# Hybrid encoder layer: the Fourier projections moved ahead of the low-rank ones, the convolution last, and a third pair of tiles for split weights

## The chip, the cores and the metric

The kernel runs on one core of a Trainium2 chip. The metric is the time of one execution in device microseconds (us). One core has five engines that matter here, each with its own in-order queue of instructions: PE (TensorE, the matrix engine), DVE (VectorE), ACT (ScalarE), POOL (GpSimd) and SP (SyncE, which here issues DMA transfers). PEld is the loading of weights into PE, which overlaps its matmuls.

## The reference

One layer on 1024 positions of 1024 channels in float32. The normalised input is projected by `w_in` to 2048 columns, which go to four groups of heads; their results are joined, projected by `w_out`, and a SwiGLU block follows.

```python
def reference(x, ...):
    h = _layer_norm(x, ln0_g, ln0_b)
    p = h @ w_in                                   # 2048 columns
    p_ssm, p_rkv, p_conv, p_fft = jnp.split(p, [256, 1024, 1792], axis=-1)
    y_a = _s5_mixer(p_ssm, ...)                    # complex state space, a scan per direction, GELU, GLU
    y_b = _rwkv7_mixer(h, p_rkv, ...)              # delta-rule scan per direction
    y_c = _short_conv_mixer(p_conv, conv_w)        # bgate * conv3(cgate * xc)
    y_d = _fourier_mixer(p_fft)                    # Re(fft2) over positions and 64 channels
    y = jnp.concatenate([y_a, y_b, y_c, y_d], axis=-1)
    h = _layer_norm(ALPHA * h + y @ w_out, ln1_g, ln1_b)
    f = (silu(h @ ffn_w1) * (h @ ffn_w3)) @ ffn_w2
    return _layer_norm(ALPHA * h + f, ln2_g, ln2_b)

# inside _rwkv7_mixer, from the normalised input xn itself:
    w_lora = tanh(xw @ w1) @ w2        # xw, xa, xg: xn mixed with its neighbours
    a = sigmoid(a0 + (xa @ a1) @ a2)
    g = sigmoid(xg @ g1) @ g2
```

## The kernel before

A scheduler orders the instructions of each engine when the program is built. The Python code gives it two streams that run beside each other. `chain()` has priority: S5, then the preparation of the RWKV scan (`rwkv_first`: `rk_prep` for both directions and both halves of the heads, then `rk_inverse(0)`, the triangular inverse of the first direction), then the scan itself (`rk_scan`, 32 steps, 16 for each direction). `beside()` fills what the chain leaves free; its parts stand in a fixed order, so that a part later in it can only come after the parts ahead of it. Once placed, an instruction keeps its place in its engine's queue: an engine whose next instruction waits does nothing else meanwhile.

Before the two streams, `start()` normalises the input, writes it transposed into eight tiles (HA and HB, the rounded part and the remainder, each in halves), and projects four blocks of 128 columns, two for S5 and two of the RWKV keys.

A projection of 128 columns is one call of `block`: the weight is loaded into `wraw` (`load`, one tile), split into a rounded part `wh` (ACT, L399) and a remainder `wl` (POOL, L400), and multiplied in two halves of 512 positions, each 48 matmuls in groups of three (L161 to L163, tile `proj`). `split` has two buffers each for `wh` and `wl` (tags WH and WL).

The parts of `beside()`:

- `lora_project`: seven projections of low-rank weights. Each weight is first multiplied by a mixing vector on DVE (L909, tile `lmw`) and the difference taken on POOL (L924). The second projection of a pair is added to the first on DVE (L925, tile `la`).
- `rkv_project`: the four other blocks for RWKV (tiles p3).
- `conv` woven with `residuals`. `conv` does, for each of two blocks, the gate C, the value, and the gate B; its DVE operations are L431 (two, product with the gate), L434 and L436 (two taps) and L438 (two, product with the other gate). `residuals` multiplies the input out again (tile `res`, L1443) and writes it to DRAM (`d_res`, L1445), eight times, through three tiles Z0, Z1, Z2.
- `fourier_project`: two projections; the first half of both, then the second half of both, into tiles C1 and C2, then to DRAM (`d_z`).
- After these `h` is not read any more, and its tiles HA0, HB0, HA1, HB1 are used as `far` for the second direction of RWKV: `rwkv_second` loads rows back from DRAM into them (L993, tiles HA0f and HB0f; HA0f and HB0f stand in HA0 and HB0), builds diagonal blocks from them (L1135, tile `abd`), multiplies (L1138, tile `pa`) and then runs `rk_inverse(1)`.

`rk_inverse` builds `ua` (L1159), and runs a loop of substitutions in which DVE and POOL each do their share (L1180, L1182), transposes (L1193, tile `tj`), and multiplies blocks (L1217, tile `pm`); then scan steps can start (matmuls `px`, `pz`, `po`, `pc`; L1303 is `pz`). When the scan of the first direction is through its 16 steps, that of the second needs `rk_inverse(1)`. The order of the parts around the change is this:

```python
for part in (self.lora_project, self.rkv_project):
    yield from part()
yield from woven((self.conv(), 0), (self.residuals(), 0))
yield from self.fourier_project()
```

## Time and profile before

| | us |
|---|---|
| time, median of 3 runs | 1436.99 |
| lowest and highest | 1435.92 and 1444.51 |
| the profiled execution, its own time | 1439.41 |
| its span in the profile | 1437.7 |
| PE busy in the span | 1324.8 (92%) |
| DVE busy | 1065.7 (74%) |
| ACT busy | 635.4 (44%) |
| POOL busy | 544.5 (38%) |

The times that follow are counted from the start of the span. The profiled execution has 1.7 us outside its span and is 2.4 us above the median. A share of 92% is a mean over stages: PE is full from 828 us to the end and has its idle time ahead of that. The stages of the table of windows below are the start (to 74.5), S5 (to 281), the preparation of the scan (to 420), the substitutions (to 461.6), the first block products (to 481.9), the first direction's steps up to the second direction's first (to 588.5), the rest of the scan (to 828), and the Fourier, output and SwiGLU matmuls.

### The profile page before, as it was taken

To read this page: it belongs to the slowest core of one execution; us is meant where nothing else is said; L and a number is where in the kernel's file an instruction comes from. 1 tells how busy PE (TensorE), PEld (TensorE's weight loads), DVE (VectorE), ACT (ScalarE), POOL (GpSimd) and SP (SyncE) were. 2 spreads that over 40 slices of the span, in tenths; PEclk is the share of its full clock that TensorE was granted. 3 is DMA by queue.
4 is the path that set the end of the run, shared out by engine and by line. 5 is a ranking of instruction groups with operands and counts; after the bars stand their busy time and mean duration, and the time that the engine had idled before them with its cause. 6 is when DMAs were issued, how large, how long until landed. Compare 5 with 4: busy or idle time off the path is not lost.

```text
span 1437.7 us, 23997 instructions
## 1 busy us (share of the span) xinstructions
PE 1324.8 (92%) x9200; PEld 1203.7 (84%) x9200; DVE 1065.7 (74%) x1882; ACT 635.4 (44%) x1249; POOL 544.5 (38%) x513
## 2 busy tenths in 40 slices
PE   6968797978799998999998999999999999999997
PEld 5968796866698877778887999999999999888885
DVE  7996967377788588678787867667666664689688
ACT  4312052565533578564338544444444454432231
POOL 5467655043356352411237443333333331122006
PEclk9989898999799999999999999999999999999999
DMA  6121024114253202405421353344444448998552
GB/s 231 36 69 27 8 94 127 45 38 121 75 163 105 108 16 96 128 27 173 158 103 59 121 175 136 140 150 162 147 147 147 148 147 297 393 354 294 190 184 117
DMA packets 94980, 196.10 MB, mean 136 GB/s; under 512 B 24721, under 2 KB 47377, under 8 KB 94865
## 3 DMA queue, kind: packets, MB, share of 16 engines
q1 hardware_dynamic: 92976, 190.74, 39.0%
q10 hardware_dynamic: 1888, 3.82, 0.8%
q8 instruction: 73, 1.20, 0.3%
q14 instruction: 43, 0.34, 0.1%
HBM read 125.32 MB, written 68.16 MB: 135 GB/s over the span
## 4 chain that ended last, share of the span: by engine, by line
PE 54%; DVE 27%; ACT 7%; DMA 5%; issue 4%; POOL 1%; SPq 1%; DVEq 0%; ACTq 0%; POOLq 0%
PE f L161 4%; PE fx L161 4%; PE f L163 4%; PE f L162 4%; PE fx L163 4%; PE fx L162 4%; PE ops L161 2%; PE ops L162 2%; PE ops L163 2%; PE fy L161 2%; PE fy L162 2%; PE fy L163 2%; DMA fw<-w 2%; PE proj L161 2%; PE proj L162 2%
## 5 line engine op out<-in xcount | busy, mean ns | idle before, releaser
L161 PE MATMUL proj<-HA,wh 128*128 128x256 f32 x672 | 201.9, 301 | 15.3 <-DVE la L925 11.1
L163 PE MATMUL proj<-HA,wl 128*128 128x256 f32 x672 | 197.3, 294 | 2.9 <-POOL wl L400 2.9
L162 PE MATMUL proj<-HB,wh 128*128 128x256 f32 x672 | 197.7, 294 | 1.7 <-POOL HB L340 1.7
L161 PE MATMUL fx<-H,fc 128*128 128x256 f32 x672 | 187.2, 283 | 2.5 <-ACT fe L1673 1.8
L162 PE MATMUL fx<-H,fc 128*128 128x256 f32 x672 | 189.5, 282 | 0.0
L163 PE MATMUL fx<-H,fc 128*128 128x256 f32 x672 | 189.0, 282 | 0.0
L1391 POOL TENSOR_TENSOR fc<-fw,fc 128x512 fp32r<-128x512 f32 x88 | 125.0, 1422 | 166.7 <-ACT fc L1390 165.8
L161 PEld LDWEIGHTS proj<-HA,wh 128*128 128x128 f32 x672 | 132.5, 197 | 22.0 <-issue 11.1
L162 PEld LDWEIGHTS proj<-HB,wh 128*128 128x128 f32 x672 | 132.4, 197 | 7.0 <-issue 4.9
L163 PEld LDWEIGHTS proj<-HA,wl 128*128 128x128 f32 x672 | 132.4, 197 | 5.8 <-POOL wl L400 3.1
L161 PEld LDWEIGHTS fx<-H,fc 128*128 128x128 f32 x672 | 126.5, 190 | 3.6 <-ACT fe L1673 2.6
L162 PEld LDWEIGHTS fx<-H,fc 128*128 128x128 f32 x672 | 127.6, 190 | 0.1
L163 PEld LDWEIGHTS fx<-H,fc 128*128 128x128 f32 x672 | 127.6, 190 | 0.0
L161 PE MATMUL f<-fb,fa 128*128 128x512 f32 x276 | 108.8, 394 | 0.0
L163 PE MATMUL f<-fb,fa 128*128 128x512 f32 x276 | 108.8, 394 | 0.0
L162 PE MATMUL f<-fb,fa 128*128 128x512 f32 x276 | 108.6, 394 | 0.0
L161 PE MATMUL fy<-H,fc 128*128 128x256 f32 x336 | 94.3, 281 | 0.4 <-ACT fe L1671 0.4
L162 PE MATMUL fy<-H,fc 128*128 128x256 f32 x336 | 94.3, 281 | 0.0
L163 PE MATMUL fy<-H,fc 128*128 128x256 f32 x336 | 94.2, 280 | 0.0
L1390 ACT CAST fc<-fw 128x512 fp32r<-128x512 f32 x110 | 67.8, 621 | 32.3 <-POOL fc L1391 14.3
L1391 POOL TENSOR_TENSOR fc<-fs,fc 128x512 fp32r<-128x512 f32 x22 | 30.1, 1369 | 105.9 <-ACT fc L1390 104.6
L1390 ACT CAST fb<-fs 128x512 fp32r<-128x512 f32 x47 | 29.1, 623 | 92.3 <-PE f L163 59.7
(634 smaller groups left out, 3794.3 us busy)
## 6 DMA issues: line engine op xcount, KB each, us to landing
fa<-d_f SPq DMA_DIRECT2D x77, 512.0 KB, 4.3
d_f<-fg SPq DMA_DIRECT2D x70, 512.0 KB, 2.7
fw<-w SPq DMA_DIRECT2D x46, 512.0 KB, 3.7
fg<-w SPq DMA_DIRECT2D x44, 256.0 KB, 6.2
wraw<-w_in SPq DMA_DIRECT2D x16, 512.0 KB, 4.1
xt<-x SPq DMA_DIRECT2D x8, 512.0 KB, 8.3
d_res<-res SPq DMA_DIRECT2D x8, 512.0 KB, 3.0
oraw<-w_out SPq DMA_DIRECT2D x8, 512.0 KB, 3.6
```

Source lines behind the costliest of these rows:

```text
L161: mm(out, whi, xhi, start=start, stop=False, skip_group_check=shared)
L162: mm(out, whi, xlo, start=False, stop=False, skip_group_check=shared)
L163: self.last_mm = mm(out, wlo, xhi, start=False, stop=stop, skip_group_check=shared)
L1390: nc.scalar.copy(out=hi, in_=raw)
L1391: (eng or nc.gpsimd).tensor_tensor(out=lo, in0=raw, in1=hi.bitcast(F32), op=ALU.subtract)
```

## The change

Four edits. The order in `beside()` becomes Fourier, low-rank, RWKV, and the convolution with the residuals last. `split` takes its tiles in turn from three places, the two buffers of WH and WL and the tiles Z0 and Z1. `fourier_project` does block after block, into P4 and P5. `residuals` has only Z2 left.

```diff
@@ build: beside()
-                        for part in (self.lora_project, self.rkv_project):
+
+                        for part in (self.fourier_project, self.lora_project, self.rkv_project):
                             yield from part()
                         yield from woven((self.conv(), 0), (self.residuals(), 0))
-                        yield from self.fourier_project()
@@ split
         if to is None:
-            hi = self.m.tile([128, NK, 128], R, tag="WH", name=self.name("wh"), bufs=2)
-            lo = self.m.tile([128, NK, 128], R, tag="WL", name=self.name("wl"), bufs=2)
+
+            self.splits += 1
+            hi, lo = (self.t(tag, [128, NK, 128], name, R)
+                      for tag, name in zip((("WH", "WL"), ("WH", "WL"), ("Z0", "Z1"))[self.splits % 3], ("wh", "wl")))
@@ fourier_project
-        z = [self.t(f"C{1 + b}", [128, S], "fz") for b in range(2)]
-        parts = [self.block(self.load(14 + b), lambda n, ps, b=b: nc.scalar.copy(
-            out=z[b][:, n * 512:(n + 1) * 512], in_=ps)) for b in range(2)]
-        for n in range(2):
-            for part in parts:
-                yield next(part)
         for b in range(2):
-            nc.sync.dma_start(out=self.d_z[b], in_=z[b])
+            z = self.t(f"P{4 + b}", [128, S], "fz")
+            yield from self.block(self.load(14 + b), lambda n, ps: nc.scalar.copy(
+                out=z[:, n * 512:(n + 1) * 512], in_=ps))
+            nc.sync.dma_start(out=self.d_z[b], in_=z)
@@ residuals
-            x = self.t(f"Z{t % 3}", [128, 2, 4, 128], "res")
+            x = self.t("Z2", [128, 2, 4, 128], "res")
```

Since the scheduler places everything anew, the order on each engine is where the change is to be seen. In the rows below a line number is that of its own program; in the changed one most are one lower (L909 is L908, L925 is L924, L1180 is L1179), and L400 is L403, L993 is L992, L440 is L443.

**VectorE in the first part of S5.** The names: `s5x`, `s5w`, `s5tt` and `s5e` are tiles of S5, `lmw` the low-rank weight times its mixing vector. Before, from the 288th row of the queue:

```order
L511 TENSOR_TENSOR s5x_86_920<-s5qin_1117,s5x_93_927 128x512 x2
L512 TENSOR_TENSOR s5x_86_920<-s5qin_1118,s5x_93_927 128x512 x2
L519 TENSOR_TENSOR s5x_93_927<-s5x_93_927 128x256
L909 TENSOR_SCALAR lmw_1348<-lraw_1346,vec 128x64 x11
L520 TENSOR_TENSOR s5x_93_927<-s5x_93_927 128x256
L519 TENSOR_TENSOR s5w_921<-s5x_86_920 128x512
...
L520 TENSOR_TENSOR s5w_922<-s5x_86_920 128x512
L909 TENSOR_SCALAR lmw_1348<-lraw_1346,vec 128x64 x5
L520 TENSOR_TENSOR s5w_922<-s5x_86_920 128x512
```

The same place in the changed program:

```order
L510 TENSOR_TENSOR s5x_84_900<-s5qin_1100,s5x_91_907 128x512 x2
L511 TENSOR_TENSOR s5x_84_900<-s5qin_1101,s5x_91_907 128x512 x2
L518 TENSOR_TENSOR s5x_91_907<-s5x_91_907 128x256
L518 TENSOR_TENSOR s5w_901<-s5x_84_900 128x512
L519 TENSOR_TENSOR s5x_91_907<-s5x_91_907 128x256
```

and, twenty rows on, where two operations of L736 stand:

```order
L734 TENSOR_TENSOR s5x_84_900<-s5qout_1102,s5x_91_907 128x1152
L735 TENSOR_TENSOR s5x_84_900<-s5qout_1103,s5x_91_907 128x1152
L736 SCALAR_TENSOR_TENSOR s5x_91_907<-s5x_84_900 128x1152
L908 TENSOR_SCALAR lmw_1629<-lraw_1627,vec 128x64 x16
L736 SCALAR_TENSOR_TENSOR s5x_91_907<-s5x_84_900 128x1152
```

The sixteen operations of `lmw` for the second pair of low-rank weights (11 and 5) have left the place between S5's own operations and stand in one piece between the two of L736 (L737 before). The two `la` operations of L925, which stood before between L735 and the second L737, are gone from there too.

**GpSimd at the substitutions of the first inverse.** The rows of L1180 and L1182 are POOL's share of the loop. Before, the loop's first rows, its middle, and what follows its end:

```order
L1166 AFFINE_SELECT ti_4280<-ua_4279 128x1024
L400 TENSOR_TENSOR wl_3699<-wraw_3696,wh_3698 128x1024
L1180 TENSOR_TENSOR tpr_4281<-ua_4279,ti_4280 128x18
...
L1180 TENSOR_TENSOR tpr_4281<-ua_4279,ti_4280 128x8x11
L400 TENSOR_TENSOR wl_3823<-wraw_3820,wh_3822 128x1024
L1182 TENSOR_TENSOR ti_4280<-ti_4280,tpr_4281 128x8x11
...
L1182 TENSOR_TENSOR ti_4280<-ti_4280,tpr_4281 128x18
L400 TENSOR_TENSOR wl_3829<-wraw_3826,wh_3828 128x1024
```

In the changed program:

```order
L1165 AFFINE_SELECT ti_4280<-ua_4279 128x1024
L1179 TENSOR_TENSOR tpr_4281<-ua_4279,ti_4280 128x18
L403 TENSOR_TENSOR wl_3813<-wraw_3810,wh_3812 128x1024
L1181 TENSOR_TENSOR ti_4280<-ti_4280,tpr_4281 128x18
...
L1181 TENSOR_TENSOR ti_4280<-ti_4280,tpr_4281 128x3x16
L403 TENSOR_TENSOR wl_3938<-wraw_3935,wh_3937 128x1024
L1179 TENSOR_TENSOR tpr_4281<-ua_4279,ti_4280 128x2x17
```

Of three remainders of weights at the loop (one ahead of it, one in it, one behind it) two are left, both inside.

**SyncE between the end of the preparation and the first scan steps.** `cg` to `d_y` is a finished block of the convolution, `res` to `d_res` a residual, HA0f and HB0f the loads of the second direction, `ring` a load of the scan. Before:

```order
L405 DMA wraw_3820<-w_in 128x1024
L405 DMA wraw_3826<-w_in 128x1024
L440 DMA d_y<-cg_3444 128x1024
L993 DMA HB0f<-d_p 128x1024
L993 DMA HA0f<-d_p 128x1024 x2
...
L1362 DMA ring_4598<-d_b 128x2x128 x2
L453 DMA d_z<-fz_3818 128x1024
```

In the changed program:

```order
L408 DMA wraw_3935<-w_in 128x1024
L1444 DMA d_res<-res_3422 128x1024
L443 DMA d_y<-cg_3105 128x1024
L1444 DMA d_res<-res_3506 128x1024
L1444 DMA d_res<-res_3528 128x1024
L1361 DMA ring_4598<-d_b 128x2x128 x2
L992 DMA HB0f<-d_p 128x1024
L992 DMA HA0f<-d_p 128x1024 x2
```

The loads into HA0f and HB0f stand behind the scan's `ring` loads now; the last reader of HA0 and HB0 ahead of them is the first half of the last convolution block instead of the first half of the second Fourier block.

## Rows read from the trace of the kernel before

**Rows 1.** Table of windows: start and end of the stretch, its length, then busy time and number of instructions of PE, PEld, DVE, ACT and POOL, the granted clock of PE as a share of full speed, the share of DMA, and GB/s. The stages.

```profile
74.50:281.00 206.50, 170.13 (x1247) 158.70 (x1247) 149.81 (x246) 57.76 (x85) 109.93 (x104) 0.91 0.21 60
281.00:420.00 139.00, 115.62 (x734) 96.34 (x732) 108.99 (x109) 77.93 (x107) 48.88 (x27) 0.90 0.33 92
...
481.90:588.50 106.60, 95.94 (x681) 81.16 (x679) 79.67 (x219) 76.55 (x214) 41.87 (x87) 0.95 0.21 69
...
828.00:1437.70 609.70, 598.19 (x4160) 556.02 (x4158) 426.47 (x580) 240.40 (x423) 179.29 (x111) 0.99 0.56 195
```

**Rows 2.** What PE waited for in the S5 stage (74.5 to 281): engine, line and tile that waited, what it waited for, us in total, times, longest.

```profile
PE proj L161 <- DVE la L925: 11.1, 3, 6.1
PE s5tp L711 <- DVE s5w L519: 10.6, 1, 10.6
PE s5py L831 <- DVE s5x L820: 10.3, 2, 8.3
PE proj L163 <- POOL wl L400: 2.9, 1, 2.9
```

**Rows 3.** Table of windows, columns as in rows 1: short stretches in which DVE is nearly full.

```profile
72.00:108.00 36.00, 22.45 (x166) 22.04 (x166) 35.85 (x131) 5.23 (x10) 23.39 (x26) 0.81 0.22 68
384.00:420.00 36.00, 31.73 (x227) 29.56 (x227) 34.52 (x45) 12.75 (x27) 13.01 (x10) 0.87 0.60 163
424.80:456.60 31.80, 31.02 (x261) 30.79 (x261) 29.84 (x67) 3.84 (x4) 22.00 (x41) 1.00 0.15 51
```

**Rows 4.** The chain of waits through S5 in order of time: start, us of the chain spent there, engine, tile and line.

```profile
98.08 1.79 DVE lmw L909 x11
...
102.68 1.14 DVE lmw L909 x3
...
104.74 1.25 DVE lmw L909 x2
...
119.30 0.61 DVE la L925
...
137.22 1.14 PE s5pv L784 x8
...
160.91 0.60 DVE la L925
...
278.08 0.86 PE pre L1035 x2
```

**Rows 5.** Table of windows, columns as in rows 1: two stretches of S5 at the low clock.

```profile
92.90:106.60 13.70, 5.73 (x27) 5.74 (x28) 13.70 (x29) 1.11 (x2) 10.32 (x9) 0.50 0.00 0
...
157.70:164.50 6.80, 2.93 (x13) 2.94 (x14) 6.77 (x5) 0.00 (x0) 6.80 (x4) 0.51 0.00 0
```

**Rows 6.** Timeline of PE in the loop of substitutions: start, us, engine, line, instruction. Between these two rows stand 18 matmuls of the same three kinds.

```profile
439.90 0.29 PE L163 MATMUL proj<-HA,wl 128*128 128x256 f32 x1
...
442.16 0.28 PE L161 MATMUL proj<-HA,wh 128*128 128x256 f32 x1
```

**Rows 7.** The chain of waits through the preparation: four operations of the first convolution block on DVE, and one mix (L1030).

```profile
389.56 1.19 DVE rav L1030
390.76 1.20 DVE cg L434
...
395.18 2.44 DVE cg L436
...
399.98 0.69 DVE cg L438
...
408.07 0.60 DVE cg L438
```

**Rows 8.** Timelines of POOL and of DVE in the loop of substitutions: start, us, engine, line, instruction. First one of POOL's remainders of weights:

```profile
435.61 2.56 POOL L400 TENSOR_TENSOR wl<-wraw,wh 128x1024 fp32r<-128x1024 f32 x1
```

and DVE's operations at the same time, with one that stands by itself and one of the convolution's:

```profile
435.48 0.41 DVE L1180 TENSOR_TENSOR tpr<-ua,ti 128x220 f32<-128x220 f32 x1
435.93 2.49 DVE L1182 TENSOR_TENSOR ti<-ti,tpr 128x220 f32<-128x220 f32 x1
...
438.83 0.68 DVE L431 TENSOR_TENSOR cz<-proj,cg 128x512 f32<-128x512 f32 x1
```

**Rows 9.** The loads of the second direction, from the view of one line: engine, transfer, count, ns of issuing (min, median, max), first and last start; then the time to landing (min, median, max).

```profile
L993 SPq DMA_DIRECT2D HB0f<-d_p x4: 326/508/843, 457.8 to 461.8; - x4
...
DMA to landing us min/median/max: 4.4/9.3/11.4
```

**Rows 10.** The chain of waits from the first block products to the second direction: columns as in rows 4.

```profile
461.59 3.70 PE pm L1217 x16
...
476.01 0.89 PE pa L1138 x8
...
505.55 1.81 PE pa L1138 x16
...
536.08 0.46 PE pz L1303 x4
...
540.38 0.46 PE pz L1303 x4
...
559.81 2.00 DVE tj L1193
```

**Rows 11.** The page's list of DMA issues: transfer, queue, count, KB each, median us from issue to landing.

```profile
d_res<-res SPq DMA_DIRECT2D x8, 512.0 KB, 3.0
```

More of the change, by code (lines that the diff above doesn't have):

```diff
@@ L144, in __init__ @@
         self.uid = 0
+        self.splits = -1
         self.parts = ("s5", "fft", "conv", "rwkv", "out")
```

## The prediction

> **What bounds the kernel now.** I read the table of windows first, because it says where PE, the engine that is busy 92% of the span, still has time to give. From 828 us to the end PE is full: 598.2 of 609.7 us [rows 1]. Nothing of the change lies there, so that stretch is taken as a block that starts earlier or later. Ahead of it the S5 stage has PE busy 170.1 of 206.5 us, which leaves 36.4 us idle, the preparation 115.6 of 139.0 (23.4 idle), and the steps of the first direction 95.9 of 106.6 (10.7 idle) [rows 1]. What counts is when the chain of S5, preparation, inverse and scan gets through these stages, together with how much PE work is done by then.
>
> Next, the waits of PE in the S5 stage say for whom it was idle: 11.1 us for `la` (L925), 10.6 us for `s5w`, 10.3 us for S5's `s5x` and 2.9 us for a split weight [rows 2]. All but the last are DVE's. The windows of DVE show why: from 72 to 108 us it is busy 35.85 of 36 us, from 384 to 420 us 34.5 of 36, and in the loop 29.8 of 31.8 [rows 3]. So up to the first `pm` at 461.6 us [rows 10] the chain is mostly DVE's, and an operation that leaves these stretches is worth its own time. The chain of waits shows which of them could: the 16 `lmw` operations take 1.79 + 1.14 + 1.25 = 4.2 us on the chain, and `la` 0.6 us each at 119.3 and 160.9 [rows 4].
>
> **The change part by part.** The price of the filling work comes first, since all of it is only moved. From the row at 439.90 us to that at 442.16 are 19 intervals: 2.26 / 19 = 0.119 us each [rows 6], so 5.7 us for a half of 48 and 11.4 us for a whole projection. The two Fourier projections are 22.8 us of PE that need nothing from DVE.
>
> *S5, to 278.* With Fourier first, PE has 22.8 us to do from 74.5 us on while DVE is full, and the low-rank weights come later. Gains: the `lmw` operations leave the full stretch (4.2 us), the two `la` near 119 us leave it too (1.2), and the 2.9 us for the first split weight go, since the first Fourier weights are split during the start. PE also falls less to its low clock. Behind its two longest pieces of idle time it ran at 0.50 of full speed, 1.2 GHz, from 92.9 to 106.6 us with 5.73 us busy, and from 157.7 to 164.5 at 0.51 with 2.93 us busy [rows 5]; at 2.4 GHz this work takes half, 2.9 and 1.5 us less. I count for the chain at its `s5pv` (137.2 us, [rows 4]) what DVE gives, 4.2 + 1.2, and for PE the clock's 2.9: about 8 us. It does not keep all. In the changed order of PE 427 matmuls of filling stand between the first direction's last `s5pv` and the second's first `s5k` where 385 stood: 42 x 0.119 = 5.0 us, of which I take 3 to lie beside DVE's work on the two scans, and 2 to be given back. The last low-rank operations (the sigmoids, the gate copies) now fall into S5's tail on ACT and DVE, among the operations that close S5; I charge 1 us, between 0 (all beside) and 4 (six operations in line at the 0.69 us of a 128x512 one, [rows 7]). S5: -5 us. Bounds: -12, when the 8 us are kept and PE's early work gives another 4; +3, when DVE's order was never the bound at `s5pv` and the tail is paid in full.
>
> *Preparation, 278 to 384.* In the changed order no RWKV projection is ahead of the end of S5; all four (rk0, 4, 1, 5) stand among the preparation's matmuls. Two mixes (L1030, on DVE) and their ACT operations (L1029, L1058) go past S5's end with them, of which the DVE part is 1.19 us each [rows 7]. PE is idle 23.4 us in this stage [rows 1], so the matmuls find room; the mixes stand on the chain. +2 us, from 0 to +5.
>
> *384 to 420.* The first convolution block's DVE operations, 1.20 + 2.44 + 0.69 + 0.60 = 4.9 us of the chain [rows 7], go from here to just ahead of the loop and into it. DVE is nearly full here, so all of it counts but for the little that filled gaps (1.5 idle of 36, [rows 3]): -4.5 us, from -4.9 to -2.
>
> *Loop, 424 to 457.* DVE's share stops while POOL writes a remainder of a weight: the L1182 at 435.93 us took 2.49 us beside a POOL L400 of 2.56, where its neighbour took 0.41 [rows 8]. Three L400 stood at the loop and two are left: one stall of 2.49 - 0.41 = 2.1 us less. The second convolution block's six operations go out of it and four of the first's come in: two L431 of 0.68 less against a slower tap, -0.8. Loop: -3 us, from -4 to +1.
>
> To this the Trainium skill (GPSIMD Engine Reference, section Specifications) has a rule: GpSimd shares its way into SBUF with VectorE, and they get in each other's way where a VectorE instruction has two SBUF inputs or runs in a two-port mode. The row of L431 agrees, 0.68 us in the middle of the loop with one input from PSUM [rows 8]. By that rule the L400 that leaves the loop would stop another two-input operation in S5 or the preparation instead, and the loop's -2.1 would be nought in the sum.
>
> At the first `pm` the sum is -5 + 2 - 4.5 - 3 = -10.5 us, bounds -21 and +7.
>
> *After the first `pm`.* Here it is paid back. In the changed order 155 matmuls of the convolution are still to come there, against 86 of Fourier before: 69 x 0.119 = 8.2 us more filling, put between block products and the first steps. PE was full from 461.6 us on, but 10.7 us are idle before 588.5 [rows 1], which can take some of it: +3, from 0 to +8. ACT and DVE do the last convolution block there too (L433, L434, L436); they share the queue with the copies behind `pm`, and I hold this inside the +3.
>
> The loads into HA0f and HB0f wait for the last reader of HA0 and HB0. Before, they were issued at 457.8 us, 3.8 us ahead of the first `pm`, and landed in 4.4 to 11.4 us [rows 9]. In the changed order that reader, the last block's first half, ends only when 107 of the 155 are done (12.7 us) and all 64 `pm` (3.7 + 1.8 + 1.8 us or so in the rows of the chain): some 20 us behind the first `pm`. The first `pa` stood 14.4 us behind `pm` (476.0, [rows 10]) and now stands among the first scan steps, behind the last convolution matmuls. Queued behind these loads on SP is little that is urgent (`ring` is ahead of them now); PE itself would wait at `pa`: +1.5, from 0 to +6.
>
> The inverse of the second direction starts later in steps: its transpose (L1193, at 559.8 us) stands behind the fifteenth step instead of the fourteenth in DVE's order. A step is 540.38 - 536.08 = 4.3 us [rows 10], and the chain then waits for this inverse, so it counts whole: +4.3, from 0 to +9 (two steps).
>
> `residuals` with one tile: the first copy of each (L1443) waits until the one before is written, 3.0 us [rows 11], against 20 to 40 matmuls (2.4 to 4.8 us) that stand between them in PE's order. Nothing, or 1 us each for the six that now run back to back in the DVE-bound stretch; PE is not the bound there, so 0 to +2.
>
> Sum: -10.5 + 3 + 1.5 + 4.3 = -1.7, about -2 us. On the profiled execution, 1439.4, that is 1437; on the median, 2.4 below it, **1435**.
>
> **The rivals.**
>
> *The idle time is really saved.* 11.1 + 10.6 + 2.9 = 24.6 us of PE's waits [rows 2] are for things that Fourier's work covers or that come early now, and 4.4 us of low clock go with them [rows 5]. If S5's chain is held more by PE's in-order queue than I think, S5 ends 12 us earlier, and the later stages keep it, since the 10.7 idle us behind `pm` take the 8.2: -21 + 4 = -17 from 1437, 1420. For it: these 24.6 are two thirds of the 36.4 idle. Against it: DVE is at 35.85 of 36 us to 108.
>
> *Slower: HA0 and HB0 come free too late.* Mechanism: the loads of the second direction wait for the last convolution half, PE's queue waits at `pa`, and the second inverse, which already held the scan back, comes later. From 457.8 to about 482 is 24 us later; from the first issue to the first `pa` were 476.0 - 457.8 = 18.2 us, of which 9.3 the load, so some 9 were free. If the other 15 us are paid and the gain to `pm` is small (-5), with the step of 4.3 and 4 of filling: 15 + 4.3 + 4 - 5 = +18, 1455. It decides from the point where the first load is issued more than some 15 us behind `pm`. Against it: the last `pa` ended 50 us after the loads were issued (507.4, [rows 10]), so the loads themselves were not what set the second inverse.
>
> *Nothing moves.* The chain in S5 follows its own scans and DMA writes, which the change leaves alone, and the paid and the saved parts are each under 5 us: 1437.
>
> **How the numbers follow.** A measurement of this kernel can tell 1% (14.4 us) from no change. My forecast of a small net has 0.45 and *nothing* 0.17; *saved* has 0.20; *slower* 0.18. The saved case and the slower one each have their far halves outside the range, which goes from 1418 to 1452. Faster by over 1% (under 1422.6) has the saved case and a little of the sum's low end, 0.21; slower (over 1451.4) 0.17; the rest, 0.62, is within 1%.
>
> **What would show it.** S5's last operation and the first `pre` at about 273 instead of 278; PE idle in the first 206 us at some 20 instead of 36 us, with no wait for `la`; the loop one stalled operation shorter; the first `pm` near 451; the second direction's first `pz` at 586 to 588, hardly earlier than 588.5, with the gap in front of it longer than before. The forecast is wrong if the first `pm` moves by more than 20 us or not at all, or if PE waits for HA0f at `pa` for more than 6 us.

## The result and the profile after

The changed kernel takes 1447.07 us (median of 13 runs, 1442.61 to 1452.92) against 1439.89 of the kernel before (13 runs): ratio 1.0055, interval 1.0043 to 1.0067. It is 0.55% slower where I forecast 1435. The time lies in the range and within the 1%, but on the other side of the kernel before, and the interval leaves "no change" out.

The profiled execution took 1446.75 us, its span is 1445.0 (1437.7 before). The page's line of busy times:

```profile
PE 1324.5 (92%) x9200; PEld 1203.1 (83%) x9200; DVE 1060.9 (73%) x1882; ACT 635.0 (44%) x1249; POOL 553.0 (38%) x513
```

PE's busy time is the same as before; all of the difference is idle time. Table of windows of the changed kernel, columns as in [rows 1], its stretches cut where the same stages end now:

```profile
74.50:280.80 206.30, 162.83 (x1206) 150.80 (x1205) 152.77 (x259) 52.47 (x79) 117.20 (x105) 0.90 0.20 61
280.80:422.70 141.90, 120.58 (x750) 100.32 (x749) 107.35 (x113) 81.86 (x111) 55.48 (x33) 0.92 0.30 88
456.00:594.70 138.70, 123.08 (x897) 108.25 (x897) 96.10 (x240) 85.81 (x232) 49.65 (x98) 0.95 0.28 93
828.00:1445.00 617.00, 604.76 (x4212) 562.17 (x4210) 427.74 (x592) 246.40 (x434) 182.47 (x111) 1.00 0.56 196
```

S5 has 206.3 - 162.8 = 43.5 us of idle PE, where 36.4 stood in [rows 1] and I had forecast 20. The preparation, here up to the start of the loop, has 21.3 idle against 23.4 (before, nothing is idle from 420 us to the loop's start at 424.9). What PE waited for in S5 (74.5 to 281), columns as in [rows 2]:

```profile
PE s5tp L710 <- DVE s5w L518: 16.6, 1, 16.6
PE proj L162 <- DVE la L924: 10.1, 1, 10.1
PE s5k L748 <- DVE s5x L736: 7.2, 1, 7.2
PE proj L162 <- DVE lg L936: 3.1, 1, 3.1
PE s5py L830 <- DVE s5x L819: 2.6, 1, 2.6
```

The wait for `la`, which I forecast to go, is still 10.1 us (11.1 in [rows 2]); it has only moved, from 120.0 and 161.6 us to 168.3. That for `s5w` has grown from 10.6 to 16.6, and a wait of `s5k` is new. The chain through the second half, columns as in [rows 4]:

```profile
451.11 2.08 DVE tj L1192
...
567.41 1.94 DVE tj L1192
...
594.74 0.49 PE pz L1302 x2
```

and the loads of the second direction, columns as in [rows 9]:

```profile
L992 SPq DMA_DIRECT2D HB0f<-d_p x4: 332/498/828, 480.7 to 484.8; - x4
...
DMA to landing us min/median/max: 3.2/8.9/10.8
```

The times of the main points, in us from the start of the span, worked out from the traces: the first `s5tp`, the first `s5k` of either S5 direction, the first `pre`, the start of the loop, the first `pm`, the second transpose `tj`, the second direction's first `pz`, and the end of the span. The rows below the first two belong to experiments; their numbers stand in front of them.

```
                            s5tp  s5k(1) s5k(2)   pre    loop    pm     tj(2)  pz(2)   end
   before                  100.9  124.2  210.2   277.9  424.9  461.6  559.8  588.5  1437.7
   after                   101.1  124.1  212.0   280.8  422.7  456.0  567.4  594.7  1445.0
 1 late_release            100.7  124.6  208.3   274.5  420.5  457.2  563.0  589.2  1439.0
 2 early_release           100.9  123.9  212.2   281.2  423.1  457.0  563.5  592.1  1444.7
 3 third_place_alone       101.0  126.3  221.1   291.8  444.9  477.8  561.5  596.1  1446.9
 4 order_alone              98.5  117.6  209.6   279.1  421.7  456.3  566.7  594.2  1442.5
 9 early_split_off_pool     98.9  121.9  210.0   279.0  420.9  454.3  563.8  591.2  1440.3
12 differences_on_dve      100.4  123.4  204.5   270.4  412.8  448.1  531.4  565.3  1416.5
13 conv_last_fourier_2nd   100.6  124.5  208.0   273.6  418.2  451.6  559.3  586.5  1437.3
15 changed_low_rank_first  100.9  126.0  219.9   289.2  438.9  469.7  565.1  599.2  1448.5
```

Each row is one execution, and such points scatter. Run 1 has the kernel before's order on PE, DVE, ACT and POOL up to 460 us, and its first `pre` came 3.4 us earlier; from there to the loop and through it the two agree within 1 us. The profiled execution of run 4 was the slowest of its seven, that of run 12 the fastest of its five.

A second sum, from the same traces, takes the span apart into PE's work at full clock, PE's idle time, and the half of its busy time at the low clock (1.2 GHz) that 2.4 GHz would have saved.

```
                            span   = work   + idle  + half of low-clock busy
   before                  1437.7   1296.2   112.9    28.6
   after                   1445.0   1294.2   120.5    30.4
 3 third_place_alone       1446.9   1292.5   120.4    34.0
 4 order_alone             1442.5   1296.9   114.6    31.0
 7 one_residual_tile       1433.4   1295.5   111.8    26.0
 9 early_split_off_pool    1440.3   1296.3   118.8    25.2
12 differences_on_dve      1416.5   1293.8    95.1    27.6
13 conv_last_fourier_2nd   1437.3   1294.1   115.5    27.8
```

The three columns add up to the span by the way they are made. What they show is that the work is 1292 to 1297 in these rows, so a difference of some 10 us or more lies in the other two; one of 4 us can't be placed by them.

**The start.** DVE's group of three small operations of S5's preparation, and POOL at the same time; before:

```profile
62.26 3.19 DVE L543 TENSOR_SCALAR xk<-xk 128x16 f32<-128x16 f32 x1
...
63.01 2.40 POOL L924 TENSOR_TENSOR lraw<-lraw,lmw 128x1024 f32<-128x1024 f32 x1
```

In the changed kernel:

```profile
62.17 5.54 DVE L542 TENSOR_SCALAR xk<-xk 128x16 f32<-128x16 f32 x1
...
62.85 2.39 POOL L403 TENSOR_TENSOR wl<-wraw,wh 128x1024 fp32r<-128x1024 f32 x1
...
65.28 2.39 POOL L923 TENSOR_TENSOR lraw<-lraw,lmw 128x1024 f32<-128x1024 f32 x1
```

The third place lets the first Fourier weight be split in the start. Its remainder (L403) stands right ahead of the low-rank difference, and DVE's small operation, which ended with the one POOL operation before, ends with the second, 5.54 - 3.19 = 2.35 us later. DVE has no time to spare there, just ahead of the full stretch of [rows 3]: in the kernel before it is busy 11.88 of 12 us (columns as in [rows 1]).

```profile
60.00:72.00 12.00, 12.00 (x103) 12.00 (x103) 11.88 (x71) 4.66 (x5) 5.92 (x15) 1.00 0.17 64
```

### The profile page after: what moved, and what is told of

Read it like the earlier page. It is cut to its first block, busy times and chain, and to the rows that moved or that the text cites. A ratio compares the mean times of both kernels' runs of the same rounds, so it can differ in the third digit from the quotient of the medians.

```text
span 1445.0 us, 24008 instructions
## 1 busy us (share of the span) xinstructions
PE 1324.5 (92%) x9200; PEld 1203.1 (83%) x9200; DVE 1060.9 (73%) x1882; ACT 635.0 (44%) x1249; POOL 553.0 (38%) x513
## 4 chain that ended last, share of the span: by engine, by line
PE 46%; DVE 15%; ACT 6%; DMA 5%; issue 3%; POOL 2%; SPq 0%; DVEq 0%; ACTq 0%; POOLq 0%
PE f L162 4%; PE f L164 4%; PE f L163 4%; PE fx L162 4%; PE fx L164 4%; PE fx L163 4%; DMA fw<-w 3%; PE ops L163 2%; PE ops L162 2%; PE ops L164 2%; PE fy L162 2%; PE fy L163 2%; PE fy L164 2%; PE pc L1322 1%; DVE fe L1652 1%
## 5 line engine op out<-in xcount | busy, mean ns | idle before, releaser
L162 PE MATMUL proj<-HA,wh 128*128 128x256 f32 x672 | 197.9, 295 | 15.5 <-DVE la L924 10.1
```

The costliest lines, as they stand in the source:

```text
L162: mm(out, whi, xhi, start=start, stop=False, skip_group_check=shared)
```

## The experiments

Medians are of runs beside runs of the kernel before on the same chip; the ratio, with its 95% interval, is to that. The scheduler places each program anew. Run 9 alone keeps the order of PE and DVE throughout; runs 1 and 2 keep it up to about the first `pm`.

**1. Late release of HA0 and HB0 in the kernel before.** The rival "HA0 and HB0 come free too late", alone: Fourier's second halves are done ahead of its first, so the last reader of HA0 and HB0 comes late.

```diff
-            out=z[b][:, n * 512:(n + 1) * 512], in_=ps)) for b in range(2)]
+            out=z[b][:, n * 512:(n + 1) * 512], in_=ps), (1, 0)) for b in range(2)]
```

> The kernel before, with one change: fourier_project runs the second half of both blocks first and the first half last, so that HA0 and HB0 are read to the very end of the projections (and HA1, HB1 come free early instead). Same matmuls, same number of instructions. In the kernel before the loads into HA0f and HB0f were issued at 457.8 us, 3.8 us ahead of the first pm; in the changed kernel at 480.7, 24.7 us behind it, and its second inverse was 7.6 us late. Theory 'release' (the late loads are what makes the second inverse late): the loads go some 15 to 20 us behind the first pm, the first pa of the second direction comes 6 to 10 us later than 475.9, the second inverse and the second direction's first pz 3 to 7 us later than 559.8 and 588.5; time 1443 to 1447 against 1439.9. Rival 'queue' (the inverse is late because its steps stand behind other work on DVE and PE, the loads have room to spare): pz within 2 us of 588.5, time 1438 to 1441.

1441.45 us, 1.0019 (1.0009 to 1.0028). The loads moved from 457.8 to 478.5 us, 20.7 later, and cost 0.19%, 2.7 us (1.3 to 4.0). That lies between the two expectations: against the 1439.9 that they start from, the theory gave 3 to 7 and the rival at most 1.

**2. Early release in the changed kernel.** The second convolution block multiplies the second half of `h` twice, so that HA0 and HB0 are free early; the kernel leaves out that block's product with the first half of `h`.

> The changed kernel, with one thing taken away: the three projections of the second convolution block read the second half of h twice instead of both halves (this computes that block's first 512 positions from the wrong input; same matmuls and instructions), so that HA0 and HB0 come free behind the first convolution block, well ahead of the first pm. Theory 'release': the loads into HA0f and HB0f are issued before the first pm, the first pa of the second direction stands 13 us or so earlier than 489.2, the second direction's first pz 5 to 8 us earlier than 594.7; time 1439 to 1443 against 1447.1. Rival 'queue': pz within 2 us of 594.7, time 1445 to 1448.

1446.36, 1.0058 (1.0044 to 1.0071), against 1.0055 of the changed kernel: no gain, with a margin of some 0.2%.

```profile
L993 SPq DMA_DIRECT2D HA0f<-d_p x4: 320/430/573, 447.2 to 451.0; - x4
```

The loads go out at 447.2 instead of 480.7, the second `tj` comes at 563.5 instead of 567.4, the second direction's first `pz` at 592.1 instead of 594.7, and the span is 1444.7 instead of 1445.0. The late release is at most a small part of the cause: the margin leaves some 2 us of it possible.

**3. Third place with one residual tile, in the old order.**

```diff
-            hi = self.m.tile([128, NK, 128], R, tag="WH", name=self.name("wh"), bufs=2)
-            lo = self.m.tile([128, NK, 128], R, tag="WL", name=self.name("wl"), bufs=2)
+            self.splits += 1
+            hi, lo = (self.t(tag, [128, NK, 128], name, R)
+                      for tag, name in zip((("WH", "WL"), ("WH", "WL"), ("Z0", "Z1"))[self.splits % 3], ("wh", "wl")))
...
-            x = self.t(f"Z{t % 3}", [128, 2, 4, 128], "res")
+            x = self.t("Z2", [128, 2, 4, 128], "res")
```

> The kernel before with only the third place for split weights (and so only Z2 for the residuals); the order of the parts and fourier_project as before. Theory 'release': the third place and the single residual tile are not what costs, HA0 comes free as before, time 1436 to 1442. Rival 'third place' (a split that comes early lies on DVE's full stretch as one more POOL subtraction, some 2.3 us in the start, and Z2 makes ACT wait): 1442 to 1447, with S5's last operation 3 us later than 278.

1448.75, 1.0069 (1.0054 to 1.0083). Windows of PE from the first `s5tp` to the first `pre`, before and here:

```profile
100.90:277.90 177.00, 154.18 (x1124) 143.91 (x1125) 123.06 (x143) 53.97 (x79) 95.28 (x87) 0.92 0.20 58
```

```profile
101.00:291.80 190.80, 164.19 (x1191) 152.84 (x1192) 128.11 (x142) 56.92 (x83) 100.15 (x88) 0.91 0.20 60
```

67 more matmuls stand in PE's queue ahead of the first `pre`, which comes 13.9 us later. More room for weights lets more filling in front of the chain. The time is above both expectations.

**4. The new order alone** (the changed kernel with two places and three residual tiles).

> The changed kernel with two places for split weights and three residual tiles as before, so that only the order (Fourier first, convolution last) and P4, P5 are changed. Theory 'release': HA0 comes free as late as in the changed kernel, time 1444 to 1449. Rival 'third place': S5 ends 3 us earlier than in the changed kernel, time 1438 to 1443.

1441.89, 1.0028 (1.0017 to 1.0039). About half of the loss is here too, as the rival expected.

**5. Third place only from the seventh split on**, so not in the start.

```diff
-                      for tag, name in zip((("WH", "WL"), ("WH", "WL"), ("Z0", "Z1"))[self.splits % 3], ("wh", "wl")))
+                      for tag, name in zip((("WH", "WL"), ("WH", "WL"), ("Z0", "Z1"))[self.splits % 3 if self.splits > 5 else 0], ("wh", "wl")))
```

> The changed kernel, but the third place is taken in turn only from the seventh split on, so that no weight can be split into it during the start. In the changed kernel a Fourier weight's remainder is written on POOL at 62.85 us, right ahead of another POOL operation, and DVE stands still for 5.54 us beside the two where it stood 3.19; the first s5tp came at 101.1 and s5k at 124.1, against 98.5 and 117.6 with two places (e4). Theory 'early split': s5tp at 98 to 99 and s5k at 117 to 119, PE idle in the whole span 3 to 6 us less than the 120.5 of the changed kernel, time 1441 to 1444 against 1447.1. Rival 'single residual tile' (what costs is that ACT waits for the residual's write, later): s5tp earlier but the time within 2 us of 1447.

1451.21, 1.0096 (1.0076 to 1.0117): worse than either expected. The early remainder is gone from the start, and the first `s5tp` comes at 98.5 us, but the scheduler placed the rest of the program anew, so this run tells nothing of its price in time.

**6. New order, two places, one residual tile.**

> The changed kernel with two places for split weights, but with the single residual tile kept: against the run e4 only the residuals' tile differs, against the changed kernel only the third place. Theory 'early split': as e4, 1441 to 1444. Rival 'single residual tile': 1445 to 1448.

1448.71, 1.0078 (1.0057 to 1.0098): by the ratios 0.5%, some 7 us, more than with three tiles (run 4), a little over what the rival expected.

**7. One residual tile alone, in the old order.**

> The kernel before with the single residual tile and nothing else; e3, with this and the third place, took 10.7 us more than before, and PE waited there 5.5 us for the residual's copies on ACT. Theory 'early split': most of e3's loss is the third place's, so this takes 1438 to 1442. Rival 'single residual tile': 1443 to 1449.

1434.21, 0.9979 (0.9966 to 0.9992), under both expectations. The same edit that costs 0.5% in the new order gains 0.2% in the old one.

**8. The mixing products `lmw` on ACT, in the kernel before.** This takes the 4.2 us of [rows 4] off DVE and leaves the order of the parts.

```diff
-                    nc.vector.tensor_scalar_mul(mw[:, k, i * step:(i + 1) * step],
-                                                raw[:, k, i * step:(i + 1) * step], self.v(mu, o + k))
+                    nc.scalar.mul(out=mw[:, k, i * step:(i + 1) * step],
+                                  in_=raw[:, k, i * step:(i + 1) * step], mul=self.v(mu, o + k))
```

> The kernel before with the multiplications of the low-rank weights by their mixing vectors (lmw, L909, 24 operations and 10.1 us of DVE in the S5 stage) on ACT, which is busy 57.8 of 206.5 us there. Theory 'PE budget': the time is PE's work plus its idle time plus what the low clock adds; s5tp comes 3 to 5 us earlier, PE's wait of 10.6 us in front of it shrinks by as much, time 1433 to 1437 against 1438. Rival 'queue': ACT's copies for the chain stand behind these operations and the gain is lost, 1437 to 1441.

1444.62, 1.0056 (1.0036 to 1.0076), above both expectations. What PE waited for in S5:

```profile
PE s5tp L711 <- DVE s5w L519: 14.0, 1, 14.0
...
PE s5k L749 <- DVE s5x L737: 9.4, 1, 9.4
```

`s5tp` comes 4.5 us earlier (96.4), as the 4.2 us say, but PE waits longer for it than before (14.0 against 10.6) and then 9.4 us more at `s5k`. An operation off DVE's full stretch moved this point of the chain earlier, and the end later. The whole schedule is new here, so the 0.56% is not the price of this edit alone.

**9. The early remainder off POOL, in the changed kernel.** The kernel leaves out the remainder of the first Fourier weight: ACT writes a copy of the weight in its place. The order on PE, DVE and SP is that of the changed kernel, row for row.

```diff
+        if to is None and self.splits == 2:
+            nc.scalar.copy(out=lo, in_=raw)
+        else:
+            nc.gpsimd.tensor_tensor(out=lo, in0=raw, in1=hi.bitcast(F32), op=ALU.subtract)
```

> The changed kernel with one operation on another engine: the remainder of the first Fourier weight, which POOL writes at 62.85 us during the start, is written by ACT instead, as a copy of the weight (so this weight's remainder is wrong; same size and type). The order of all instructions on PE, DVE and SP is the same row by row. Theory 'early split': DVE stands still for 3.2 us instead of 5.54 beside POOL at 62 us, s5tp comes 2 to 2.5 us earlier than 101.1, PE's wait of 16.6 us in front of it shrinks by as much, and since all later queues are the same, time falls by 1.5 to 2.5, to 1444.5 to 1445.5. Rival 'nothing': another wait takes its place and the time stays within 1 us of 1447.

1442.65, 1.0030 (1.0018 to 1.0042). Timelines of DVE and POOL, then PE's wait:

```profile
62.34 3.19 DVE L545 TENSOR_SCALAR xk<-xk 128x16 f32<-128x16 f32 x1
...
63.10 2.40 POOL L926 TENSOR_TENSOR lraw<-lraw,lmw 128x1024 f32<-128x1024 f32 x1
```

```profile
PE s5tp L713 <- DVE s5w L521: 14.3, 1, 14.3
```

The small operation is back at 3.19 us, PE's wait is 2.3 us shorter, every point up to the first `pm` is 1.7 to 2.2 us earlier, and the second direction's first `pz` 3.5. By the ratios it is worth 0.25%, 3.6 us; with the two intervals that is some 1 to 6, so it is not told from the 2.35 us of DVE. In the second sum idle time fell by 1.7 us and the low-clock column by 5.2 (30.4 to 25.2); why the latter is not settled. This is the one run that takes a single cause out of the changed kernel and holds the order of PE and DVE.

**10 to 12. Remainders, then low-rank differences, on DVE.** If POOL's subtractions hold DVE for their 2.4 us, DVE should do them itself. Run 10 does the remainders so in the changed kernel, run 11 in the kernel of run 7, run 12 adds the differences (L924, L936) to run 11.

```diff
-        nc.gpsimd.tensor_tensor(out=lo, in0=raw, in1=hi.bitcast(F32), op=ALU.subtract)
+        eng = nc.vector if to is None and self.splits > 1 else nc.gpsimd
+        eng.tensor_tensor(out=lo, in0=raw, in1=hi.bitcast(F32), op=ALU.subtract)
```

> The changed kernel with the remainders of all weights but those of the start written by DVE (one 128x1024 subtraction, estimated at 1.2 to 1.4 us from the other two-input operations of that size) instead of POOL (2.4 us, during which DVE's two-input operations stand still). Theory 'shared way': DVE loses 1.3 us for each where it lost up to 2.1, and PE's first s5tp and the loop come 1 to 4 us earlier; time 1440 to 1446 against 1447.1. Rival 'DVE is the bound': each adds 1.3 us to DVE where it is full and nothing is gained, 1447 to 1453.

1430.8, 0.9949 (0.9933 to 0.9965), better than expected.

```profile
L404 DVE TENSOR_TENSOR wl<-wraw,wh x12: 1199/1222/3207, 59.5 to 421.5; 128x1024 fp32r<-128x1024 f32 x12
...
L404 POOL TENSOR_TENSOR wl<-wraw,wh x2: 2536/2686/2837, 11.7 to 22.4; 128x1024 fp32r<-128x1024 f32 x2
```

The same subtraction is 1.22 us on DVE and 2.69 on POOL (the two left there).

> The kernel of e7 (before with the single residual tile, 1434.2) with the remainders of all weights but those of the start written by DVE instead of POOL. Theory 'shared way': 1429 to 1434. Rival 'DVE is the bound': 1434 to 1440.

1425.96, 0.9924 (0.9902 to 0.9946), under the expected range too.

> The kernel of e11 (1426.0) with the three differences of low-rank weights (L924 and L936, 128x1024, 2.4 to 2.8 us on POOL) on DVE as well. Theory 'shared way': the one in the start stops DVE for 3.2 us now and takes it 1.3 then, so s5tp comes some 2 us earlier; time 1421 to 1426. Rival 'DVE is the bound': 1426 to 1430.

1422.48, 0.9892 (0.9869 to 0.9915): the best of all, faster than both kernels, with every part of the work done. Its gain over run 11 is about as large as the two intervals. The page's line of busy times:

```profile
PE 1321.5 (93%) x9200; PEld 1201.2 (85%) x9200; DVE 1052.8 (74%) x1904; ACT 634.4 (45%) x1249; POOL 498.9 (35%) x491
```

DVE has 22 instructions more than in the changed kernel and is busy less (1052.8 against 1060.9; 1065.7 before): what it no longer stands for POOL is more than what it took over. All its other operations are those of the kernel before. At 1.22 us each the 22 take 27 us, so by this estimate the others take 1065.7 - 1052.8 + 27 = 40 us less, which fits operations of DVE that stood beside POOL before. PE's idle time falls to 95.1 us in the second sum. The schedules of runs 10 to 12 are new, so how much of their gain is the hold and how much the placing is not separated.

**13. Low-rank first, Fourier second, convolution last** (two places, three residual tiles).

```diff
-                        for part in (self.fourier_project, self.lora_project, self.rkv_project):
+                        for part in (self.lora_project, self.fourier_project, self.rkv_project):
```

> The order low-rank, Fourier, RWKV, convolution last, with two places for split weights and three residual tiles. It keeps the low-rank weights where the kernel before has them, in front, and has the convolution last as the changed kernel. The theory that the new order costs its 3.9 us (1441.9 with the same tiles) by what lies behind the first block products, where the convolution's matmuls and its DVE operations stand: 1441 to 1444, the first pm near 456 and the second inverse's transpose at 563 or later. The rival, that the cost comes from the low-rank part standing later, among S5's second scan and its close: 1436 to 1439, as the kernel before.

1439.77, 1.0009 (0.9997 to 1.0022). Beside run 4 only the place of Fourier differs: with it in front 1.0028, with it second no difference from the kernel before that the interval shows. So with two places the convolution at the end costs at most some 3 us, and the low-rank part behind Fourier some 2.7 (0.19%, with an interval of about 0.02 to 0.36). Both schedules are new. Where the time goes: the first `pre` is at 273.6 here and at 279.1 in run 4. What DVE waited for from 245 to 282 in run 4, with one low-rank operation there:

```profile
DVE s5w L871 <- ACT s5xw L870: 9.0, 3, 7.1
...
L948 DVE TENSOR_TENSOR lg<-lb 32x1024 f32<-32x1024 f32 x1 | 2.9, 2876 | 0.6 <-ACT lb L945 0.6
```

and from 244 to 276 here, where no low-rank operation is left:

```profile
DVE s5w L871 <- ACT s5xw L870: 4.6, 3, 3.0
```

From the last group of `s5py` (246.3 us in run 4, 245.2 here) to the first `pre` are 32.8 us in run 4 and 28.4 here.

**14. Fourier split**, one block in front and one last.

> The first Fourier projection stands in front, the second one last, the convolution ahead of it as in the kernel before; two places for split weights, three residual tiles. The theory that the convolution at the end costs: 1436 to 1439, since the convolution is back ahead of the first block products and only one Fourier projection (11.4 us) stands behind them. The rival, that Fourier in front of the low-rank part costs: half of it or more stays, 1440 to 1443, with the first pre later than 278.

1452.39, 1.0085 (1.0067 to 1.0102), above both ranges; the first `pre` is at 277.1, so the loss is behind S5 (the loop starts at 429.3 against 424.9). It does not tell the two theories apart.

**15. The changed kernel with the low-rank part in front again**, the rest as changed.

> The changed kernel with one thing undone: the low-rank part stands in front of Fourier again; the third place, the one residual tile and the convolution last stay. The theory that Fourier in front costs some 5 us because the last low-rank operations then fall into S5's second scan and close (first pre 273.6 with low-rank first, 279.1 with Fourier first, both with two places): 1440 to 1443, the first pre 4 us or more ahead of 280.8. The early remainder stays in the start here (now of a low-rank weight), so its 3.6 us stay. The rival, that with three places the order makes no difference: 1445 to 1448.

1452.91, 1.0113 (1.0099 to 1.0128), above both. It looks like run 3: with three places and the low-rank part in front the first `pre` is at 289.2, with 1734 matmuls ahead of it (1748 in run 3, 1655 in the changed kernel). So the share of the order in the changed kernel itself can't be read from run 13 alone.

**16 and 17. The order of run 13 with run 12's edits**, with three residual tiles and with one.

> Low-rank, Fourier, RWKV, convolution last, two places, three residual tiles, with the weights' remainders and the low-rank differences on DVE. From 1439.8 of the same order with them on POOL, and the 11.7 us that the same move gave the kernel with one residual tile (1434.2 to 1422.5): 1426 to 1430.

1427.62, 0.9928 (0.9906 to 0.995), as expected.

> As the run before, and one residual tile. If the one tile gives here what it gave the kernel before (2.9 us): 1423 to 1427; if its waits fall on PE in this order, as they did with Fourier in front (1441.9 to 1448.7): 1430 or more.

1426.13, 0.9924 (0.9911 to 0.9937), as expected. Neither reaches run 12.

## Why the prediction was wrong

Forecast and measured, in us against the kernel before, by the prediction's own terms (from the table of points):

```
                            forecast   measured
S5, to the first pre          -5         +2.9
preparation and 384 to 420    -2.5       -5.1
loop                          -3         -3.4
behind the first pm           +8.8      +12.9
sum                           -1.7       +7.3
```

The measured column compares two executions. Against run 1's, which has the same order up to 460 us, S5 would be 6.3 us longer and not 2.9; the next two rows would differ by 1 us at most.

**The step that failed is S5's -5**: the runs showed +2.9 in its place, 7.9 us off, just inside the upper bound of +3. Within it, it is the term *"for the chain at its `s5pv` ... about 8 us"*: the first `s5pv` came at 136.4 us where 137.2 stood, 0.9 earlier (2.9 in run 9, at 134.3). The 3 us that the prediction gave back from there to the first `pre` were 3.8. The part of the 8 that was PE's clock did not come either. From 74.5 to 142 us PE's granted clock was 0.87 of full speed before and 0.82 in the changed kernel, with fewer matmuls done (columns as in [rows 1], before and changed):

```profile
74.50:142.00 67.50, 48.54 (x367) 47.29 (x366) 54.94 (x146) 13.75 (x22) 45.06 (x36) 0.87 0.13 35
...
74.50:142.00 67.50, 43.21 (x330) 41.76 (x329) 56.69 (x152) 11.81 (x21) 45.31 (x39) 0.82 0.22 68
```

The parts of the step:

- *"The first Fourier weights are split during the start"* was counted as a gain of the 2.9 us wait alone. What POOL's remainder does to DVE there was put at nothing, though [rows 8] show a DVE operation stand 2.49 us beside one, and though the paragraph behind the loop's term says that a remainder which leaves the loop would stop an operation of S5 or the preparation instead. It named the effect and gave it no term and no chance. Run 9: 2.35 us of DVE, and 3.6 us (1 to 6) of the kernel.
- *"The `lmw` operations leave the full stretch"* is right, but only the eleven ahead of the first `s5tp`, 1.79 of the 4.2 us [rows 4], could move that point, and the early remainder took 2.35: `s5tp` came at 101.1 where 100.9 stood. And the operations did not go to a place that hides them. Timeline of DVE in the changed kernel, and of POOL:

```profile
117.45 3.29 DVE L735 TENSOR_TENSOR s5x<-s5qout,s5x 128x1152 f32<-128x1152 f32 x1
120.78 3.18 DVE L736 SCALAR_TENSOR_TENSOR s5x<-s5x 128x1152 f32<-128x1152 f32 x1
123.88 2.68 DVE L908 TENSOR_SCALAR lmw<-lraw,vec 128x64 f32<-128x64 f32 x16
126.48 1.34 DVE L736 SCALAR_TENSOR_TENSOR s5x<-s5x 128x1152 f32<-128x1152 f32 x1
...
119.49 3.25 POOL L735 TENSOR_TENSOR s5x<-s5qout,s5x 128x1152 f32<-128x1152 f32 x1
```

  Before, DVE waited 3.56 us for POOL ahead of the second of these L737:

```profile
127.19 1.36 DVE L737 SCALAR_TENSOR_TENSOR s5x<-s5x 128x1152 f32<-128x1152 f32 x1 [3.56 <-POOL s5x L736]
```

  Now the place is full: two operations of 1.3 us take 3.2 and 3.3 beside POOL's, and the 2.68 us of `lmw` come on top.
- *"PE has 22.8 us to do while DVE is full"*: PE did less there. By `s5tp` it had done 536 matmuls (557 before), since the scheduler put `s5tp` further ahead in PE's queue; PE waits for it 16.6 us with Fourier's work queued behind. Filling helps only when it stands ahead of the wait in the queue.
- *The tail*, charged 1 us with bounds 0 to 4: run 4 against run 13 gives 32.8 - 28.4 = 4.4 us for the same close of S5 with the last low-rank operations in it and without. In the changed kernel itself it is 31.5, against 30.3 before, so there the charge of 1 us was right. More was lost just ahead of it: from the second direction's `s5tp` to its `s5k` are 212.0 - 193.2 = 18.8 us, against 210.2 - 194.7 = 15.5 before.

**The preparation and the loop** were right in sign, the first undersized. Two remainders are left in the loop, each with one stalled operation, as the prediction said. Timeline of DVE:

```profile
422.87 2.50 DVE L1181 TENSOR_TENSOR ti<-ti,tpr 128x30 f32<-128x30 f32 x1
...
440.56 2.42 DVE L1181 TENSOR_TENSOR ti<-ti,tpr 128x180 f32<-128x180 f32 x1
```

The row of L431 that the prediction reads as agreeing with the rule is no test of it: it began at 438.83, when the remainder (435.61 + 2.56) was over. A better pair stands in the same trace. Beside one remainder an operation with an input from PSUM (L925) kept its 0.68 us, and the next one, with both inputs in SBUF (L520), waited for the remainder's end:

```profile
168.51 0.68 DVE L925 TENSOR_TENSOR la<-proj,lb 128x512 f32<-128x512 f32 x1
169.11 2.27 DVE L520 TENSOR_TENSOR s5w<-s5x 128x512 f32<-128x512 f32 x1
...
168.33 2.51 POOL L400 TENSOR_TENSOR wl<-lraw,wh 128x1024 fp32r<-128x1024 f32 x1
```

**Behind the first `pm`** the pay-back is 12.9 instead of 8.8. The stretch from there to the second direction's first `pz` was, before (columns as in [rows 1]):

```profile
461.60:588.50 126.90, 116.23 (x828) 101.46 (x828) 88.08 (x233) 86.20 (x233) 48.08 (x98) 0.93 0.27 93
```

In the changed kernel (456.00 to 594.70 above) PE does the 69 matmuls more that were forecast and is busy 123.08 - 116.23 = 6.9 us longer, where +3 was charged because idle time would take the rest. The idle time took nothing: it grew from 10.7 to 15.6 us. The second `tj` comes 567.4 - 559.8 = 7.6 us later, where the first `pm` is 5.6 earlier. I blamed a step for 4.3 of it, which is not tested; run 2 takes the late loads away, by which it comes 4 us earlier, and gains nothing at the end that its margin shows.

**The chain's points do not all carry the end.** The second transpose does not: run 2 moves it by 4 us with no gain. Nor does the first `pm`: run 5 has it where the kernel before has it (461.7 us) and ends 10 us later in its profile. The last point of the chain does. From the second direction's first `pz` to the end of the span are 847.9 to 853.3 us in all nineteen profiles, the two kernels and the seventeen runs, while that `pz` itself lies between 565.3 and 605.5. So summing the chain up to it was sound; its terms were off. PE's idle and low-clock time take the whole span apart after the fact, and do not say which wait a change will lengthen.

Of the rivals, *slower: HA0 and HB0 come free too late* gave the right sign by a mechanism that runs 1 and 2 do not bear out as the main cause: 21 us of delay cost 0.2% where it forecast 15 us, undoing it gives nothing clear of the margin, and in the changed kernel's trace PE stands idle ahead of no `pa`.

**What stays open.** Of the 7 us, 3.6 (1 to 6) are the early remainder. The rest is as large as what the order alone costs with two places (1441.89), and run 13 puts most of that on the low-rank part behind Fourier. But run 15, which should have shown it in the changed kernel, came out slower still, because three places let more filling ahead of the chain when the low-rank part is in front (runs 3, 15). The edits don't add: order alone +0.28%, third place with one tile +0.69%, one tile alone -0.21%, all together +0.55%. Each new set of constraints gives another schedule, and such runs don't price one edit within another. The cause of about half of the loss is open.

## What to carry to other kernels

Before counting a moved operation as gained, look at what shares its new place: here a POOL subtraction that came early by a spare buffer held DVE for its whole 2.4 us. Where a scheduler replans, an experiment proves a cause only if the order of the engines stays as it was, as in run 9. Find the last point of the chain from which the end follows at a fixed distance, here the second direction's first `pz`, and judge a change by what moves that point; an earlier one can move by 4 us for nothing. A busy engine may be standing: if DVE is full and POOL's two-input operations run beside it, try those on DVE.

## What the runs showed of the hardware

I had not expected that moving POOL's subtractions of 128x1024 onto the engine that bounds the stretch would be a gain: 1.22 us on DVE against 2.4 to 2.7 on POOL, and 1447.07 to 1430.8 us for the kernel. The Trainium skill (GPSIMD Engine Reference, section Engine selection) tells to do element-wise work on VectorE, GpSimd being about twice as slow for two inputs; the rows of run 10 agree, 2.69 / 1.22 = 2.2.

Nor that a group of three DVE operations of 128x16, of which the first has one input, stood 5.54 us through two POOL operations in a row. The Trainium skill (VectorE: DVE Perf Modes, section Mode 2×_2P) says that an operation with one input in SBUF may use both read ports; the row of L542 fits that, but does not show which of the three was held.
